# Low-half products of the first MLP half woven between the high-half products

## The chip, the cores and the metric

The kernel runs on one core of a Trainium2 chip. The metric is the device time of one execution in microseconds. Names used below: TensorE multiplies matrices (PE in the profile, with its weight loads on a row of their own, PEld), VectorE is DVE, ScalarE is ACT, GpSimd is POOL, and SyncE (SP) issues the loads from memory.

## The reference

One layer of a diffusion backbone: two token mixers (differential attention and multi-scale pooling) merged by gates, and then a squared-ReLU MLP. There are 256 latent tokens and 256 context tokens of 2048 channels; the MLP has 8192 hidden channels. Everything is in float32. What matters here is the last line:

```python
def sq_relu_mlp(h, w1, w2):
    return jnp.square(jax.nn.relu(h @ w1)) @ w2

x = x + ga * mix
x = x + gm * sq_relu_mlp(modulate(x, norm_mlp_w[l], sm, cm), w_ff1[l], w_ff2[l])
```

## The kernel before

**High and low halves.** TensorE multiplies in the type float32r, which keeps fewer bits than float32. So every operand is split in two: `hi` is the value rounded to float32r, `lo` the rounded rest, `value - hi`. A product of two float32 matrices is then three products: high by high, high by low, and low by high. Weights arrive in chunks of 128 x 1024 values in one of five `raw` tiles, by a DMA on SyncE's queue. ScalarE casts a chunk to `whi` (line 243, `act.copy(hi, raw)`), VectorE subtracts to get `wlo` (line 244); there are three `whi` and three `wlo` tiles. `wchunk` hands out the next chunk of a long list, `stream`, whose order is written out beforehand, and sees to it that two chunks beyond it have been asked for (`AHEAD = 2`). At a certain rate it also advances a side job, `late_gen`, which works out a modulation vector from weights of its own: it borrows a `raw` tile for each of them, and VectorE multiplies and adds it into `macc` (line 651).

**The MLP.** The hidden channels are worked through in eight blocks of 1024, numbered 0 to 7. `ff1_first` makes block 0. `ff1(b)` makes block b for 1 to 7 and `ff2(b)` multiplies the finished block with its part of the second weight matrix and adds to `acc`. They are called in the order `ff1(1)`, `ff2(0)`, `ff1(2)`, `ff2(1)`, and so on to `ff1(7)`, `ff2(6)`, `ff2(7)`. So a block that `ff1` finishes is read only one `ff2` later.

**`ff1`.** The weights are the stationary operand, 128 x 128 at a time, and the hidden state `h2` moves. For each of the block's eight columns of 128 channels (four pairs `i`, two halves `j`) there is one PSUM bank `ps` of 512 columns and there are two chunks of weights (`kc`), each with eight slices `kk`. Per chunk there are first eight high products: `both(h2, k)` is the high and the low half of `h2` side by side, 2 x 256 = 512 columns, so that one product gives high by high in the bank's first 256 columns and high by low in its last 256. Behind them come eight low products: the slice of `wlo` with the high half of `h2` alone, 256 columns, added to the bank's last 256. These are lines 1061 and 1064 (below called highs and lows). After both chunks ScalarE copies the last 256 columns out (`f1c`, line 1067) and VectorE adds the first 256 (`f1s`, line 1068). After two columns ScalarE takes the ReLU, GpSimd squares, and `split` (lines 270, 271) makes the high and low half of the block, `act`.

**`ff2` and the other stages.** `xstat` makes the products of `ff2` and of most other projections: the tokens are stationary, the weights move, 512 columns a product. Per chunk it gives, for `part == 0`, the high weights with the high and the low half of the tokens (lines 453 and 454, alternating), and for `part == 1` the low weights with the high half (line 459). In `ff2` that is eight and four products a chunk. The pooling stage uses `mm3` (lines 274 to 276) with products of 256 columns.

**Order.** The instructions are scheduled from the order of the text; on TensorE the profile shows the products of the MLP in the order of the text. Functions handed to `later` are called some chunks on, from `wchunk`.

Of the kernel before, what the change touches and what calls it, by code (L numbers as in the profile page):

```python
# [13 lines left out]
AF = mybir.ActivationFunctionType  # L14
# [3 lines left out]
P = 128  # L18
D = 2048
KT = D // P  # L20
T = 256
# [27 lines left out]
def layer(ctx: ExitStack, tc, a, out):  # L49
# [3 lines left out]
    pe, gp = nc.tensor, nc.gpsimd  # L53
# [15 lines left out]
    act, vec, pe, sp = Engine(nc.scalar, ordered), Engine(nc.vector, ordered), Engine(nc.tensor, ordered_pe), nc.sync  # L69

    def bank(name):
        return psum.tile([P, 512], F32, tag="ps", name=name)

    def work(name, shape=None, dt=F32):
        return pool.tile(shape or [P, 512], dt, tag="w2", name=name, bufs=9)

    def s16(name, shape, dt=F32):
        return pool.tile(shape, dt, tag="s16", name=name, bufs=7)
# [7 lines left out]
    def pairtile(name):  # L86
        return s16(name, [P, 2, 8, T], F32R)
# [8 lines left out]
    def later(n, fn):  # L96

        waiting.append([n, fn])
# [154 lines left out]
    def wchunk(*key, ahead=AHEAD):  # L253
        while len(loaded) < min(done[0] + 1 + ahead, len(stream)) or loaded[done[0]][1] is None:
            if loaded and done[0] < len(loaded) and loaded[done[0]][1] is None:
                done[0] += 1
                continue
            load_next()
        got, hi, lo = loaded[done[0]]
        assert got == key, (got, key)  # L260
        loaded[done[0]] = None
        done[0] += 1
        tick()
        return hi, lo
# [4 lines left out]
    def split(hi, lo, src):  # L269
        act.copy(hi, src)  # L270
        vec.tensor_sub(lo, src, hi.bitcast(F32))  # L271

    def mm3(o, l_hi, l_lo, r_hi, r_lo, start, stop):
        pe.matmul(o, l_hi, r_hi, start=start, stop=False)
        pe.matmul(o, l_hi, r_lo, start=False, stop=False)
        pe.matmul(o, l_lo, r_hi, start=False, stop=stop)
# [89 lines left out]
    def act_slice(tiles, k, part):  # L366
        return tiles[k // 8][:, part, k % 8, :]

    def both(tiles, k):
        return tiles[k // 8][:, :, k % 8, :]  # L370

    def tok(tiles, k, part, t):
        return tiles[k // 8][:, part, k % 8, t * P:t * P + P]
# [56 lines left out]
    def xmm(banks, toks, k, hi, lo, sl, first, last):  # L430
        for ps, (h, t) in zip(banks, toks):
            mm3(ps, tok(h, k, 0, t), tok(h, k, 1, t), hi[:, sl], lo[:, sl], first, last)

    def xstat(w, banks, toks, nk=8, last=1, more=0, held_back=None):

        for ch in range(nk - last + 1):
            n = last if ch == nk - last else 1  # L440
            chunks = [wchunk(*w, ch + i, ahead=max(AHEAD - i, more if i == last - 1 else 0)) for i in range(n)]
            order = [(i, kk, t) for i in range(n) for kk in range(2) for t in range(len(banks))]
            if ch == nk - last:
                order.sort(key=lambda o: o[2])
            groups = [order] if n == 1 else [[o for o in order if o[2] == t] for t in range(len(banks))]
            for group in groups:
                for part in range(2):
                    for i, kk, t in group:
                        k = 2 * (ch + i) + kk
                        h, tt = toks[t]  # L450
                        wt = chunks[i][part][:, kk * 512:kk * 512 + 512]
                        if part == 0:
                            pe.matmul(banks[t], tok(h, k, 0, tt), wt, start=k == 0, stop=False)  # L453
                            pe.matmul(banks[t], tok(h, k, 1, tt), wt, start=False, stop=False)  # L454
                        elif held_back is not None and group is groups[-1] and k >= 2 * nk - 3:
                            held_back.append(partial(pe.matmul, banks[t], tok(h, k, 0, tt), wt, start=False,
                                                     stop=k == 2 * nk - 1))
                        else:
                            pe.matmul(banks[t], tok(h, k, 0, tt), wt, start=False, stop=k == 2 * nk - 1)  # L459
            yield len(banks)  # L460
# [110 lines left out]
    for f in range(KT):  # L571
        if f % 2 == 0:
            ps = bank("mod")
# [109 lines left out]
    def v_group(g):  # L683
        bs = [bank(f"v{g}_{t}") for t in range(4)]
        for ch, w in enumerate(xstat(("w_v", g), bs, tokens(4))):

            yield w if g == 0 or ch > 1 else 2 * ch
        for t in range(4):
            act.copy(v[:, t, g * 512:g * 512 + 512], bs[t])
        values[0] += 4  # L690

    def k_group(g):
        bs = [bank(f"k{g}_{t}") for t in range(4)]
        for ch, w in enumerate(xstat(("w_k", g), bs, tokens(4))):
            if ch < 7:
                yield w
        for t in range(4):
            qk_evac(bs[t], t, g, kT, 2, 3 + t)
        yield w

    def q_group(g):
        bs = [bank(f"q{g}_{t}") for t in range(2)]
        for _ in xstat(("w_q", g), bs, tokens(2)):
            yield 0
        for t in range(2):
            qk_evac(bs[t], t, g, qT, 0, 4 + t)
# [243 lines left out]
    h2 = [pairtile("h2_0")]  # L950
# [25 lines left out]

    acc = s16("acc", [P, 2, D])
    acts = {}

    def ff1_first(wo):  # L980

# [54 lines left out]
        for h in range(2):  # L1036
# [5 lines left out]
                part.append(r)  # L1042
            later(3 + h, partial(turn4, at, 4 * h, part))

    def ff1(b):

        at = pairtile("act")  # L1050
        acts[b] = at
        for i in range(4):
            s = work("f1s")
            for j in range(2):
                f = 8 * b - 8 + 2 * i + j
                ps = bank("f1")
                for kc in range(2):
                    hi, lo = wchunk("w_ff1", f, kc)
                    for kk in range(8):
                        k = 8 * kc + kk  # L1060
                        pe.matmul(ps, hi[:, kk * P:kk * P + P], both(h2, k), start=k == 0, stop=False)  # L1061
                    for kk in range(8):
                        k = 8 * kc + kk
                        pe.matmul(ps[:, T:2 * T], lo[:, kk * P:kk * P + P], act_slice(h2, k, 0), start=False,  # L1064
                                  stop=k == KT - 1)
                c = work("f1c", [P, T])
                act.copy(c, ps[:, T:2 * T])
                vec.tensor_add(s[:, j * T:j * T + T], ps[:, 0:T], c)
            sq = work("rsq2")
            r = work("relu")  # L1070
            act.activation(r, s, AF.Relu)  # L1071
            gp.tensor_mul(sq, r, r)  # L1072
            split(at[:, 0, 2 * i:2 * i + 2, :], at[:, 1, 2 * i:2 * i + 2, :], sq.rearrange("p (a t) -> p a t", t=T))

    def ff2(b):
        at = [acts[b]]
# [20 lines left out]
    for b in range(8):  # L1097
        if b < 7:
            ff1(b + 1)
        else:  # L1100
            for g in range(4):
                gs = slice(g * 512, g * 512 + 512)
                for t in range(2):
                    gp.tensor_mul(acc[:, t, gs], acc[:, t, gs], mods["gm"][:, gs])
                    gp.tensor_add(acc[:, t, gs], acc[:, t, gs], x1[:, t, gs])
        ff2(b)
# [105 lines left out]
```

## Time and profile before

| what | value |
| --- | --- |
| median of 3 runs | 1470.62 us (1469.34 to 1471.14) |
| the profiled execution's own time | 1469.82 us |
| its span, first to last instruction | 1467.8 us |
| mean granted TensorE clock | 0.994 |
| TensorE busy (page, part 1) | 1437.1 us, 98% of the span |
| weight loads busy | 1183.6 us, 81% |
| VectorE, ScalarE, GpSimd busy | 1000.2, 683.5, 121.3 us |
| first line-1061 product to last (timeline) | 798.5 to 1374.9 us |

The page gives, in part 1, the time in which an engine was busy; in part 4 the chain of work that ended last, followed back from the end; in part 5 the costliest groups of instructions with their count, their busy time, the mean duration of one, and the engine's idle time before them. Durations of products overlap, because TensorE starts one before the last has drained: what a product costs is the distance from its start to that of the next. In the page a line such as `f<-h,whi` names the tile written and the tiles read; `ps` and `bs` of the MLP carry the name `f` there.

### The profile page before, as it was taken

What the parts mean: (1) busy time and instruction counts of PE and PEld (TensorE: products, weight loads), DVE (VectorE), ACT (ScalarE), POOL (GpSimd) and SP (SyncE); (2) the same over time, 40 slices, a digit from 0 to 9 for tenths busy, and PEclk for the clock granted to TensorE, in tenths of its full rate; (3) what the DMA queues carried; (4) which work ended last, traced back from release to release, by engine and by line L of the source; (5) the groups of instructions that cost most, each with busy time, mean ns of one, the idle gap of its engine ahead of it and who ended that gap; (6) DMA issues with size and microseconds to landing.
All of it is one profiled execution on the core that took longest, in us unless ns stands there. A gap on an engine that the chain in (4) does not pass through costs nothing.

```text
span 1467.8 us, 19774 instructions
## 1 busy us (share of the span) xinstructions
PE 1437.1 (98%) x7466; PEld 1183.6 (81%) x7466; DVE 1000.2 (68%) x1243; ACT 683.5 (47%) x929; POOL 121.3 (8%) x120
## 2 busy tenths in 40 slices
PE   4999999999999999999999999999999999999998
PEld 3667887778878888888888888888888888888887
DVE  4667787868887786768676656666666655555675
ACT  4334336466554344435444554445344453544442
POOL 0001110101400000000001000001000000000260
PEclk8999999999999999999999999999999999999999
DMA  9996585435788888899646777767777655555554
GB/s 364 409 408 237 198 284 178 144 115 167 226 289 293 297 274 305 279 310 323 206 168 204 231 245 233 238 224 235 238 239 241 201 189 193 191 190 194 185 195 141
DMA packets 97439, 347.85 MB, mean 237 GB/s; under 512 B 11072, under 2 KB 11712, under 8 KB 97344
## 3 DMA queue, kind: packets, MB, share of 16 engines
q1 hardware_dynamic: 96768, 345.51, 69.6%
q8 instruction: 58, 0.95, 0.3%
q0 software_dynamic: 576, 1.08, 0.2%
q14 instruction: 37, 0.30, 0.1%
HBM read 344.45 MB, written 2.10 MB: 236 GB/s over the span
## 4 chain that ended last, share of the span: by engine, by line
PE 91%; DVE 4%; ACT 2%; DMA 1%; issue 1%; POOL 0%; DVEq 0%; SPq 0%; ACTq 0%; POOLq 0%
PE f L1061 14%; PE f L454 8%; PE f L453 8%; PE f L459 8%; PE f L1064 7%; PE pg L454 4%; PE pg L453 4%; PE pg L459 4%; PE w_k L67 3%; PE wo L453 2%; PE wo L454 2%; PE pyy L453 2%; PE pyy L459 2%; PE pyy L454 2%; PE wo L459 2%; PE v L459 2%
## 5 line engine op out<-in xcount | busy, mean ns | idle before, releaser
L244 DVE TENSOR_TENSOR wlo<-raw,whi 128x1024 fp32r<-128x1024 f32 (+1 forms) x430 | 534.7, 1245 | 341.6 <-ACT whi L243 319.6
L243 ACT CAST whi<-raw 128x1024 fp32r<-128x1024 f32 (+1 forms) x430 | 449.6, 1047 | 551.7 <-PE f L454 179.6
L1061 PE MATMUL f<-h,whi 128*128 128x512 f32 x896 | 224.3, 392 | 0.0
L454 PE MATMUL f<-whi,act 128*128 128x512 f32 x512 | 199.3, 389 | 0.0
L453 PE MATMUL f<-whi,act 128*128 128x512 f32 x512 | 199.3, 389 | 0.0
L1061 PEld LDWEIGHTS f<-h,whi 128*128 128x128 f32 x896 | 161.6, 189 | 29.2
L651 DVE SCALAR_TENSOR_TENSOR macc<-raw,sil,macc 128x1024 f32<-128x1024 f32 x128 | 165.0, 1289 | 4.0 <-issue 2.5
L459 PE MATMUL f<-wlo,act 128*128 128x512 f32 x512 | 136.8, 389 | 0.0
L1064 PEld LDWEIGHTS f<-h,wlo 128*128 128x128 f32 x896 | 122.2, 190 | 8.7
L1064 PE MATMUL f<-h,wlo 128*128 128x256 f32 x896 | 124.9, 282 | 0.0
L459 PEld LDWEIGHTS f<-wlo,act 128*128 128x128 f32 x512 | 96.1, 188 | 20.0
L454 PEld LDWEIGHTS f<-whi,act 128*128 128x128 f32 x512 | 96.1, 188 | 19.8
L453 PEld LDWEIGHTS f<-whi,act 128*128 128x128 f32 x512 | 96.1, 188 | 19.8
L453 PE MATMUL pg<-whi,hL 128*128 128x512 f32 x256 | 101.4, 396 | 0.0
L454 PE MATMUL pg<-whi,hL 128*128 128x512 f32 x256 | 100.6, 393 | 0.0
L1072 POOL TENSOR_TENSOR rsq<-relu 128x512 f32<-128x512 f32 x28 | 29.2, 1043 | 527.5 <-ACT relu L1071 497.0
L459 PE MATMUL pg<-wlo,hL 128*128 128x512 f32 x256 | 68.6, 390 | 0.0
L454 PEld LDWEIGHTS pg<-whi,hL 128*128 128x128 f32 x256 | 48.5, 189 | 10.3 <-issue 0.2
L453 PEld LDWEIGHTS pg<-whi,hL 128*128 128x128 f32 x256 | 48.5, 189 | 10.3 <-issue 0.2
L459 PEld LDWEIGHTS pg<-wlo,hL 128*128 128x128 f32 x256 | 48.4, 189 | 10.1
L632 POOL MEMSET macc<- 128x1024 f32 x8 | 7.6, 955 | 479.2 <-DVE al L271 374.9
L1086 DVE TENSOR_TENSOR acc<-f,acc 128x512 f32<-128x512 f32 x48 | 30.9, 686 | 19.6 <-PE f L459 19.6
(275 smaller groups left out, 2098.1 us busy)
## 6 DMA issues: line engine op xcount, KB each, us to landing
raw<-in_w_ff_dram SPq DMA_DIRECT2D x240, 512.0 KB, 4.2
raw<-in_w_m_dram SPq DMA_DIRECT2D x64, 512.0 KB, 9.8
raw<-in_w_ga_dram SPq DMA_DIRECT2D x32, 512.0 KB, 4.6
raw<-in_w_cm_dram SPq DMA_DIRECT2D x32, 512.0 KB, 4.6
raw<-in_w_gb_in_dram SPq DMA_DIRECT2D x32, 512.0 KB, 4.7
raw<-in_w_ga_in_dram SPq DMA_DIRECT2D x32, 512.0 KB, 5.0
raw<-in_w_sm_dram SPq DMA_DIRECT2D x32, 512.0 KB, 4.9
raw<-in_w_o_dram SPq DMA_DIRECT2D x32, 512.0 KB, 4.6
```

What stands on the lines that cost most here:

```text
L67: return (lambda *a, **k: pin(emit(*a, **k))) if self.flag[0] else emit
L243: act.copy(hi, raw)
L244: vec.tensor_sub(lo, raw, hi.bitcast(F32))
L453: pe.matmul(banks[t], tok(h, k, 0, tt), wt, start=k == 0, stop=False)
L454: pe.matmul(banks[t], tok(h, k, 1, tt), wt, start=False, stop=False)
L459: pe.matmul(banks[t], tok(h, k, 0, tt), wt, start=False, stop=k == 2 * nk - 1)
L632: gp.memset(acc, 0.0)
L651: pin(vec.scalar_tensor_tensor(acc, raw, sil[:, 0, k:k + 1], acc, ALU.mult, ALU.add))
L1061: pe.matmul(ps, hi[:, kk * P:kk * P + P], both(h2, k), start=k == 0, stop=False)
L1064: pe.matmul(ps[:, T:2 * T], lo[:, kk * P:kk * P + P], act_slice(h2, k, 0), start=False, stop=k == KT - 1)
L1072: gp.tensor_mul(sq, r, r)
L1086: vec.tensor_add(acc[:, t, gs], bs[t], acc[:, t, gs])
```

## The change

The lows of `ff1` are no longer given out in runs of eight. Each is put into a list, `behind`, as its high is given out, and `weave(4)` gives out the oldest entry when the list holds more than four. So behind the first four highs of a block, high and low alternate, and each low comes four highs after the high of its own slice. This goes on across chunks and columns. The last four lows of a block are still in the list when `ff1` ends; `xstat`, in the `ff2` that follows, calls `weave(0)` behind each of its products with `part == 0`, and so they stand behind the first four of those. Elsewhere the list is empty and `weave` does nothing. What followed a column's last low (copy, addition, and after two columns ReLU, square and split) has moved into `ff1_out` and is given out behind that low, wherever it now stands. The number of instructions, their shapes and the list of loads are the same.

```diff
+    behind = []
+
+    def weave(lag):
+
+        if len(behind) > lag:
+            behind.pop(0)()
+
     def xstat(w, banks, toks, nk=8, last=1, more=0, held_back=None):
...
                             pe.matmul(banks[t], tok(h, k, 0, tt), wt, start=k == 0, stop=False)
+                            weave(0)
                             pe.matmul(banks[t], tok(h, k, 1, tt), wt, start=False, stop=False)
+                            weave(0)
...
+    halves = [None]
+    LAG = 4
...
+    def low_product(ps, lo, kk, k, done_with):
+
+        pe.matmul(ps[:, T:2 * T], lo[:, kk * P:kk * P + P], act_slice(h2, k, 0), start=False, stop=k == KT - 1)
+        if k == KT - 1:
+            done_with()
+
+    def ff1_out(b, i, j, ps):
+
+        if j == 0:
+            halves[0] = work("f1s")
+        s = halves[0]
+        c = work("f1c", [P, T])
+        act.copy(c, ps[:, T:2 * T])
+        vec.tensor_add(s[:, j * T:j * T + T], ps[:, 0:T], c)
+        if j == 1:
+            at = acts[b]
+            sq = work("rsq2")
+            r = work("relu")
+            act.activation(r, s, AF.Relu)
+            gp.tensor_mul(sq, r, r)
+            split(at[:, 0, 2 * i:2 * i + 2, :], at[:, 1, 2 * i:2 * i + 2, :], sq.rearrange("p (a t) -> p a t", t=T))
+
     def ff1(b):
-        at = pairtile("act")
-        acts[b] = at
+        acts[b] = pairtile("act")
         for i in range(4):
-            s = work("f1s")
             for j in range(2):
...
                         pe.matmul(ps, hi[:, kk * P:kk * P + P], both(h2, k), start=k == 0, stop=False)
-                    for kk in range(8):
-                        k = 8 * kc + kk
-                        pe.matmul(ps[:, T:2 * T], lo[:, kk * P:kk * P + P], act_slice(h2, k, 0), start=False,
-                                  stop=k == KT - 1)
-                c = work("f1c", [P, T])
-                act.copy(c, ps[:, T:2 * T])
-                vec.tensor_add(s[:, j * T:j * T + T], ps[:, 0:T], c)
-            sq = work("rsq2")
...
+                        behind.append(partial(low_product, ps, lo, kk, k, partial(ff1_out, b, i, j, ps)))
+                        weave(LAG)
```

More of the change, by code (lines that the diff above doesn't have):

```diff
@@ L1061, in ff1 @@
                         pe.matmul(ps, hi[:, kk * P:kk * P + P], both(h2, k), start=k == 0, stop=False)
-                    for kk in range(8):
-                        k = 8 * kc + kk
-                        pe.matmul(ps[:, T:2 * T], lo[:, kk * P:kk * P + P], act_slice(h2, k, 0), start=False,
-                                  stop=k == KT - 1)
-                c = work("f1c", [P, T])
-                act.copy(c, ps[:, T:2 * T])
-                vec.tensor_add(s[:, j * T:j * T + T], ps[:, 0:T], c)
-            sq = work("rsq2")
[L1070 to L1073, printed above, removed]
+                        behind.append(partial(low_product, ps, lo, kk, k, partial(ff1_out, b, i, j, ps)))
+                        weave(LAG)
     def ff2(b):
```

## The prediction

> **What bounds the kernel now.** I read the page first, for the share of each engine and the costliest groups; then the chain of waits around one block of the first MLP half; then the timeline, product by product, where a run of short products begins and ends.
>
> ```profile
> span 1467.8 us, 19774 instructions
> PE 1437.1 (98%) x7466; PEld 1183.6 (81%) x7466; DVE 1000.2 (68%) x1243; ACT 683.5 (47%) x929; POOL 121.3 (8%) x120
> ...
> PE 91%; DVE 4%; ACT 2%; DMA 1%; issue 1%; POOL 0%; DVEq 0%; SPq 0%; ACTq 0%; POOLq 0%
> ...
> L1061 PE MATMUL f<-h,whi 128*128 128x512 f32 x896 | 224.3, 392 | 0.0
> ...
> L1064 PE MATMUL f<-h,wlo 128*128 128x256 f32 x896 | 124.9, 282 | 0.0
> ```
>
> TensorE is busy 98% of the span and carries 91% of the chain that ended last. The two lines that the change moves, 896 high products of 512 columns and 896 low ones of 256, have no idle time before them. So the time of this stage is the sum of the distances from one product's start to the next. The mean durations (392 and 282 ns) overlap and say nothing of that; the chain of waits does. It is merged here for the stretch 885 to 940 us (start, length, line, count; its times lie 0.16 us behind the starts of the timeline, so only differences are used):
>
> ```profile
> 885.85 0.23 PE f L453
> ...
> 888.57 1.81 PE f L1061 x8
> 890.38 0.95 PE f L1064 x8
> 891.34 1.84 PE f L1061 x8
> 893.17 0.95 PE f L1064 x8
> ...
> 930.44 1.84 PE f L1061 x8
> 932.28 0.95 PE f L1064 x8
> 933.24 0.23 PE f L453
> ```
>
> Between 885.85 and 888.57 lie the twelve 512-column products of one chunk of the second MLP half: 2.72 us, or 226.7 ns each. Eight of that rate make 1.81 us, which is what the block's first eight highs take. Every later run of eight highs takes 1.84 us, and each run of eight lows 0.95 us, 119 ns each. One chunk (eight and eight) takes (930.44 - 891.34) / 14 = 2.793 us, or 349.1 ns for a pair of one high and one low.
>
> If a low took half of a high by its columns, it would take 113.3 ns, a pair 340.0 ns, a chunk 2.720 us. So 0.073 us of each chunk is lost. Where, the timeline of single products shows (start, length, engine, line; each of these rows is the answer to a narrow window, and a row of two starts at its first):
>
> ```profile
> 889.99 0.39 PE L1061 MATMUL f<-h,whi 128*128 128x512 f32 x1
> 890.22 0.28 PE L1064 MATMUL f<-h,wlo 128*128 128x256 f32 x1
> 890.33 0.40 PE L1064 MATMUL f<-h,wlo 128*128 128x256 f32 x2
> 890.45 0.40 PE L1064 MATMUL f<-h,wlo 128*128 128x256 f32 x2
> 890.57 0.40 PE L1064 MATMUL f<-h,wlo 128*128 128x256 f32 x2
> ...
> 890.22 0.19 PEld L1064 LDWEIGHTS f<-h,wlo 128*128 128x128 f32 x1
> 890.34 0.19 PEld L1064 LDWEIGHTS f<-h,wlo 128*128 128x128 f32 x1
> 890.45 0.19 PEld L1064 LDWEIGHTS f<-h,wlo 128*128 128x128 f32 x1
> ...
> 933.07 0.40 PE L453 MATMUL f<-whi,act 128*128 128x512 f32 x1
> ...
> 934.23 0.39 PE L454 MATMUL f<-whi,act 128*128 128x512 f32 x1
> ```
>
> The low that follows a high lasts 0.11 us (890.22 to 890.33); from the second on they last 0.12. Each weight load starts as the product before its own starts (load 890.22 beside product 890.22, load 890.34 beside product 890.33). So a load has exactly one product's length to hide in: behind a high it has 227 ns, behind a low 113. Back to back behind lows it takes 120, about 7 ns too much, seven times in a run: 0.047 us. The rest, 0.026 us, is the run of highs that follows (1.84 against 1.81): a high after a run of lows is slow for a while. The same is seen in the second half behind the block: five products from 933.07 to 934.23 take 1.16 us instead of 5 x 0.2267 = 1.133.
>
> **The change part by part.** Instructions, shapes and counts are the same; only the order of TensorE's products changes, and with it the moment at which buffers come free.
>
> Order: behind the first four highs of a block, high and low alternate; the last four lows of a block stand behind the first four products of the second half that follows. No low follows a low any more. The price of a pair is not in the trace as an alternating stream, so I bound it. From below: a high at its best rate (226.7) and a low at its best (113.3), 340.0 ns; no row above is faster. From above, the only place where highs stand between short products: two lone 512-column products inside the pooling's runs of 256 columns.
>
> ```profile
> 331.53 0.28 PE L276 MATMUL pin<-hL,wlo 128*128 128x256 f32 x1
> 331.65 0.40 PE L670 MATMUL late<-ah,ones 128*128 128x512 f32 x1
> 331.88 0.40 PE L671 MATMUL late<-al,ones 128*128 128x512 f32 x1
> 332.12 0.28 PE L274 MATMUL pin<-hL,whi 128*128 128x256 f32 x1
> 332.24 0.28 PE L275 MATMUL pin<-hL,whi 128*128 128x256 f32 x1
> 332.36 0.28 PE L276 MATMUL pin<-hL,wlo 128*128 128x256 f32 x1
> ```
>
> Those two take (332.12 - 331.65) / 2 = 235 ns, the 256s behind them 120: a pair of 355 ns, worse than the 349.1 of today. I take the lower end, 340. The reason is the row at 890.22: there a low stands behind a high that is at its best rate, as it does in the new order, and it takes 113. Behind the low comes a high whose load began as the low began, just as the load at 890.22 began, and that one was in time. The pooling's highs stand behind a run of 256s that had been waiting for their loads, a state which the new order never enters.
>
> The sum at that rate: fifteen chunks of a block give 0.073 each and the first, which has no slow highs, 2.77 - 2.72 = 0.05 (891.34 - 888.57), together 1.14 us; seven blocks 8.0 us. The slow products behind the seven blocks give 7 x 0.027 = 0.2. Gain 8.2 us. The profiled execution took 1469.82 us (its span and 2.0 us around it), so 1461.6 by its own measure; the median of the runs is 0.8 us above it, so 1462.4.
>
> Buffers: the last high of a chunk now begins 2.4 us into it instead of 1.6, so the cast that waits for the freed high tile (890.42 below, as the eighth high of its chunk ends) comes 0.8 us later. The last low ends 1.4 us into the next chunk (after three pairs, a high and itself), so the subtraction that fills the freed low tile starts at 1.4 us into that chunk, not 0.3. These hide behind work that is in the rows:
>
> ```profile
> 890.42 1.05 ACT L243 CAST whi<-raw 128x1024 fp32r<-128x1024 f32 x1 [0.70 <-PE f L1061]
> ...
> 888.78 1.23 DVE L244 TENSOR_TENSOR wlo<-raw,whi 128x1024 fp32r<-128x1024 f32 x1 [1.50 <-ACT whi L243]
> ...
> 890.04 0.33 SPq L116 DMA_DIRECT2D raw<-in_w_ff_dram  x1
> ...
> raw<-in_w_ff_dram SPq DMA_DIRECT2D x240, 512.0 KB, 4.2
> ...
> 898.80 1.05 ACT L243 CAST whi<-raw 128x1024 fp32r<-128x1024 f32 x1 [1.74 <-PE f L1061]
> ...
> 888.40:933.00 44.60, 44.60 (x257) 39.26 (x256) 28.66 (x30) 23.09 (x32) 3.13 (x3) 1.00 0.73 236
> ```
>
> With three buffers, a tile filled in the chunk after its release is read two chunks later. The subtraction would end at 1.4 + 1.2 = 2.6 us, the first low that reads it is at 2 x 2.72 + 1.6 = 7.0 us: 4.4 us to spare. What queues behind that subtraction on VectorE (the f1s additions, the accumulations of the late modulation) is read by nobody on TensorE for as long; VectorE is busy 28.66 of the block's 44.60 us and ScalarE 23.09. The raw buffer is released at the subtraction's end, and SyncE issues its next load at once (888.78 + 1.23 = 890.01, issue 890.04). It lands about 4.2 us later, at 894.2, and with five raw buffers, one of them lent to the late weights, its cast is the fourth from there, at 898.80: 4.6 us to spare, of which the later release takes 1.1. So SyncE's queue is moved by a microsecond and no cast waits for it. The copy, addition, ReLU and square of each column block come 1.4 us later; their PSUM bank is held that much longer, with eight banks and three or four in use. At a block's end they fall into the second half, and their result is read a whole stage (over 40 us) later. I cost all of this at nothing; if the cover were gone, each microsecond per chunk would cost 112 us.
>
> **A page weighed against a row.** In a run of lows the trace shows one load per 120 ns. The Trainium skill, "TensorE: Matmul & The Clock Gate", section "LDWEIGHTS (loading the stationary operand)", gives a load as its columns divided by 1.2, which is 107 ns for 128 columns. By that estimate a load fits into a low's 113 ns and the sum is the 8.2 us above; by the 120 of the row, if it holds behind a single low too, it is the second rival below. The same page, section "Step-by-step: what each phase is for", says that loads are pulled ahead into a background weight buffer; the loads of this trace, each starting with the product before its own, agree, and this speaks against the change: a low is too short to hide more than one load, wherever it stands.
>
> **The rivals.** First, on the other side: the highs never get back to their best rate. Each high stands behind a low, and every row of a high behind a run of lows is slow, as at 331.65. With 355 ns a pair the stage takes 896 x (355 - 349.1) = 5.3 us more: 1475.9. It decides as soon as a pair costs over 349.1. For it speaks that recovery took five highs at 933.07, and the new order never has two highs in a row; against it, that all such rows stand behind lows that had waited for loads.
>
> Second: the load of a high's weights needs 120 ns behind its low, as the loads at 890.34 and 890.45 do, while the highs keep 226.7. Pair 346.7, gain 896 x (349.1 - 346.7) = 2.2 us: 1468.4, no measurable change. Against it: the first low's 0.11.
>
> Third: the order on the chip isn't that of the text, because the lows find another place when the instructions are scheduled, or the two effects cancel: 1470.6. The order of before agrees with its text row by row (x8, x8), which speaks against.
>
> Fourth: a new wait. If the subtraction, now behind the last low, came 4.4 us too late, TensorE would stand; 0.1 us a chunk is 11.2 us, 1473.6 with the gain kept. The sums above speak against it.
>
> **How the numbers follow.** What a measurement here can tell from no change is about 0.2%, 2.9 us. The forecast has 0.46 (its own range 1461.0 to 1465), the slow highs 0.22, the bound load 0.20, no other order or a cancellation 0.08, a wait 0.04. Faster is the forecast alone, 0.46; same is the bound load and the third rival, 0.28; slower is the first and the fourth, 0.26. The range goes from the forecast by its best case, 1461.0, to the slow highs at 1476.0; beyond lies little but the wait.
>
> **What would show it.** In the chain of waits the runs x8 of both lines are gone, and a high and a low take 0.34 us together, 5.44 us for sixteen pairs; 0.347 is the bound load, 0.35 and above the slow highs. A block (now 933.24 - 888.57 = 44.67 us) takes 43.5. The high after a low is 0.227 apart from its successor if I am right, 0.233 to 0.236 if the first rival is. The first five products of the second half lose their 0.027. The idle time before both product lines stays 0.0; if not, a wait has come. The prediction is wrong if the slow state belongs to any change of length rather than to waiting loads.

## The result, and the profile after

The changed kernel takes 1473.48 us (median of 11 runs, 1471.13 to 1476.17); the kernel before took 1468.92 us in 11 runs beside them. The ratio is 1.0026, 95% interval 1.0015 to 1.0036: slower by a quarter of a per cent, some 3.8 us (the medians differ by 4.6), where 1462.4 was forecast. The profiled execution took 1473.48 us, with a span of 1471.5.

The page after, for the same groups as before, by engine, line, tile and shape, with count, busy time, mean ns of one, and idle time before it:

```profile
span 1471.5 us, 19748 instructions
PE 1441.5 (98%) x7466; PEld 1182.3 (80%) x7466; DVE 1000.3 (68%) x1243; ACT 685.1 (47%) x929; POOL 145.0 (10%) x120
...
L1089 PE MATMUL f<-h,whi 128*128 128x512 f32 x896 | 313.5, 398 | 0.0
L1058 PE MATMUL f<-h,wlo 128*128 128x256 f32 x896 | 251.6, 281 | 0.0
```

Lines 1089 and 1058 are the highs and lows that were lines 1061 and 1064. Their idle time is still 0.0: no wait has come. The whole loss is in the distances between products. The timeline of the same block shows them (start, length, engine, line):

```profile
889.83 0.28 PE L1058 MATMUL f<-h,wlo 128*128 128x256 f32 x1
889.94 0.40 PE L1089 MATMUL f<-h,whi 128*128 128x512 f32 x1
890.17 0.28 PE L1058 MATMUL f<-h,wlo 128*128 128x256 f32 x1
890.29 0.40 PE L1089 MATMUL f<-h,whi 128*128 128x512 f32 x1
890.53 0.28 PE L1058 MATMUL f<-h,wlo 128*128 128x256 f32 x1
890.65 0.40 PE L1089 MATMUL f<-h,whi 128*128 128x512 f32 x1
890.88 0.28 PE L1058 MATMUL f<-h,wlo 128*128 128x256 f32 x1
891.00 0.40 PE L1089 MATMUL f<-h,whi 128*128 128x512 f32 x1
...
892.06 0.40 PE L1089 MATMUL f<-h,whi 128*128 128x512 f32 x1
```

The order is the one in the text. But it repeats itself every three pairs: from 889.94 to 891.00, and again to 892.06, three highs and three lows take 1.06 us, 353.3 ns a pair. Before it was 349.1, and 340 was forecast. 896 x (353.3 - 349.1) = 3.8 us, which is the loss: the two profiled spans differ by 3.7. In the trace's nanoseconds the three highs take 232, 241 and 235, the lows behind them 118, 120 and 114; none of these highs takes 227. Behind the last low of the block the second half is slow as well (chain of waits; start, length, line):

```profile
934.97 0.24 PE f L460
935.21 0.24 PE f L462
...
935.68 0.23 PE f L462
```

So the 0.2 us that the forecast counted there did not come either. The slow stretch even grew: by the starts in the traces it costs 63 ns over ten products behind six of the seven blocks, where it cost 27 ns over five before.

The buffers moved about as worked out. In the chunk that starts with the high at 891.00, the cast and the subtraction are:

```profile
893.91 1.05 ACT L243 CAST whi<-raw 128x1024 fp32r<-128x1024 f32 x1 [1.77 <-DVE wlo L244]
...
892.66 1.23 DVE L244 TENSOR_TENSOR wlo<-raw,whi 128x1024 fp32r<-128x1024 f32 x1 [2.37 <-PE f L1058]
```

The cast comes 2.9 us into its chunk, as its last high ends (893.87 in the trace); before it came 2.0 us in (a chunk from 888.41, the cast at 890.42). The row puts the wait down to the subtraction, which ends at nearly the same moment, 893.89. With the lag of one, below, the subtraction ends at 894.05 and the cast, at 894.58, is put down to the high; so it is the high that it waits for. The subtraction waits for TensorE's last low of the chunk ahead, 1.66 us into this one.

One delay was not foreseen. GpSimd's square takes 1894 ns on the page after, 1043 on the page before; ScalarE's cast of its result waits for it, up to 2.2 us at a time, and a cast of weights queued behind that one comes late (at 906.66, though the high in its way ended at 905.17). TensorE doesn't feel it: its idle time is 0.0, and the run with short loads for the highs, below, has the square at 1850 ns and is fast all the same.

### The profile page after: what moved, and what is told of

It reads as the page before. It is cut to its first block, busy times and chain, and to the rows that moved or that the text cites. A ratio compares the mean times of both kernels' runs of the same rounds, so it can differ in the third digit from the quotient of the medians.

```text
span 1471.5 us, 19748 instructions
## 1 busy us (share of the span) xinstructions
PE 1441.5 (98%) x7466; PEld 1182.3 (80%) x7466; DVE 1000.3 (68%) x1243; ACT 685.1 (47%) x929; POOL 145.0 (10%) x120
## 4 chain that ended last, share of the span: by engine, by line
PE 87%; DVE 6%; DMA 3%; ACT 2%; issue 1%; POOL 0%; SPq 0%; DVEq 0%; ACTq 0%; POOLq 0%
PE f L1089 14%; PE f L460 8%; PE f L462 8%; PE f L468 8%; PE f L1058 7%; PE pg L460 3%; PE pg L462 3%; PE pg L468 3%; PE w_k L67 2%; PE wo L460 2%; PE wo L462 2%; PE wo L468 2%; PE pyy L462 2%; PE pyy L468 2%; PE pyy L460 2%; PE v L462 2%
## 5 line engine op out<-in xcount | busy, mean ns | idle before, releaser
L1089 PE MATMUL f<-h,whi 128*128 128x512 f32 x896 | 313.5, 398 | 0.0
L1058 PE MATMUL f<-h,wlo 128*128 128x256 f32 x896 | 251.6, 281 | 0.0
L1089 PEld LDWEIGHTS f<-h,whi 128*128 128x128 f32 x896 | 168.4, 188 | 41.7
L1058 PEld LDWEIGHTS f<-h,wlo 128*128 128x128 f32 x896 | 169.2, 189 | 0.3
L1075 POOL TENSOR_TENSOR rsq<-relu 128x512 f32<-128x512 f32 x28 | 53.0, 1894 | 510.6 <-ACT relu L1074 410.7
L271 DVE TENSOR_TENSOR act<-rsq,act 128x512 fp32r<-128x512 f32 x28 | 19.4, 693 | 44.4 <-ACT act L270 44.4
```

## The experiments

Times of single runs stand beside one run of the kernel before on the same chip, or beside the median of nine, and differ by a few microseconds from run to run. So the verdicts rest on the distances in the traces, which repeat. "Short" is a load of 64 stationary columns instead of 128.

**Is it the alternation of tiles and banks?** Lows of 512 columns:

```diff
-        pe.matmul(ps[:, T:2 * T], lo[...], act_slice(h2, k, 0), start=False, stop=k == KT - 1)
+        pe.matmul(ps, lo[...], both(h2, k), start=False, stop=k == KT - 1)
```

> The order of the changed kernel, with lows of 512 columns (the low weights times both halves of the hidden state), so that every product of the stage has the same length and only the tile of the weights alternates. Theory R (rhythm: a product is slow behind one of another length, whatever the loads do): all products settle at 226.7 ns, a pair at 453.3, time 1468.9 + 896 x (453.3 - 349.1) ns = about 1562 us. Theory L (load: a high is slow because its weights had to be loaded beside a short low): the same 453.3, since every load has 227 ns. Theory T (tiles or bank: taking turns between high and low weight tiles, or adding to a part and to the whole of a bank, costs by itself): at least the 13 ns a pair lost in the changed kernel stay, 467 ns, about 1574 us.

1563.59 us against 1472.54. The chain of waits:

```profile
904.78 0.23 PE f L1058
905.00 0.23 PE f L1089
...
906.82 0.23 PE f L1089
```

Nine products from 904.78 to 906.82 take 2.04 us, 226.7 ns each, highs and lows alike. Taking turns between two weight tiles costs nothing. Here the lows write the whole bank too, so this run says nothing of turns between the whole and a part of a bank; the next one does, where highs write the whole and lows a half, and lose nothing. The two together put theory T out. Theories R and L expected the same and are not told apart.

**Is it the high's load?** Woven order, 64 stationary columns in 15 of 16 highs:

```diff
+                        m = P if k == 0 else 64
-                        pe.matmul(ps, hi[:, kk * P:kk * P + P], both(h2, k), ...)
+                        pe.matmul(ps[0:m, :], hi[:, kk * P:kk * P + m], both(h2, k), ...)
```

> The order of the changed kernel, but 15 of 16 highs use 64 of their 128 stationary columns (half of the output channels are left out), so that the load that must fit beside a low is halved. Theory L: the load is in time and the pair falls from 353.3 to 340 ns, time about 1461 us. Theory R: lengths alternate as before, the pair stays near 353 ns, about 1473 us.

1463.65 us against 1472.54. Its timeline, with the one full load among sixteen at 909.34 (128*128); the last row is that load:

```profile
909.00 0.39 PE L1090 MATMUL f<-h,whi 128*64 128x512 f32 x1
909.23 0.28 PE L1058 MATMUL f<-h,wlo 128*128 128x256 f32 x1
909.34 0.40 PE L1090 MATMUL f<-h,whi 128*128 128x512 f32 x1
909.57 0.28 PE L1058 MATMUL f<-h,wlo 128*128 128x256 f32 x1
909.69 0.39 PE L1090 MATMUL f<-h,whi 128*64 128x512 f32 x1
909.92 0.28 PE L1058 MATMUL f<-h,wlo 128*128 128x256 f32 x1
910.03 0.39 PE L1090 MATMUL f<-h,whi 128*64 128x512 f32 x1
...
910.71 0.39 PE L1090 MATMUL f<-h,whi 128*64 128x512 f32 x1
...
909.23 0.19 PEld L1090 LDWEIGHTS f<-h,whi 128*128 128x128 f32 x1
```

With the short load a pair takes the 340 ns of the forecast (909.00 to 909.34; two pairs from 910.03 to 910.71 in 0.68), although lengths alternate: theory L expected this, theory R 353. And the fully loaded high shows how the loss is paid. The low in front of it, beside which its load ran, is as short as ever, 0.11 (909.23 to 909.34). What comes after is slow: the high and the low behind it take 0.35 (909.34 to 909.69), and the two pairs to 910.03 take 0.69; in the trace's nanoseconds 693 instead of 680, spread over the high (232), the low (118) and the next high (230). So here the late load does not hold back the start of its product; it makes the product itself, and the two behind it, longer. (A product with 64 stationary columns also uses half of the array. No run halves the load alone in float32r, but such products are no faster by themselves: with both at 64, in the next runs, a pair still takes 340 ns, which is the 226.7 of a full product of 512 columns and half of that.)

The other way round, 64 columns in the lows and 128 in the highs (`m = P if k == KT - 1 else 64` at the lows), and both at 64:

> The order of the changed kernel; now 15 of 16 lows use 64 of their 128 stationary columns (half of their channels left out) and the highs keep 128, so that the shorter load is the one beside a high. Theory S (share: every load takes time from the stream of the product beside it, in proportion to its columns, 13.3 ns for 128 and 6.7 for 64, wherever it stands): high 220, low 120, pair 340 ns, 8 us below the kernel before. Theory L (only the high's load beside the short low does harm): nothing changes for it, the pair stays at 353 ns, 4 us above. Theory R (unlike lengths alone): 353 as well, but the run with highs of 64 columns, at 340, already speaks against it.

> As the run with lows of 64 stationary columns, with 15 of 16 highs at 64 too. Theory S: high 220, low 113.3, pair 333.3 ns, 14 us below the kernel before. Theory L: all loads are in time, high 226.7 and low 113.3, pair 340, 8 us below.

1466.09 and 1461.85 us against 1469.09. From the chain of waits of the two, first the short lows alone, then both:

```profile
904.92 0.12 PE f L1059
905.04 0.23 PE f L1090
...
907.35 0.12 PE f L1059
```

```profile
905.01 0.11 PE f L1059
905.12 0.23 PE f L1091
...
906.71 0.11 PE f L1059
```

Seven pairs in 2.43 us are 347 ns, five pairs in 1.70 are 340. Short loads for both are no faster than short loads for the highs alone. So the load beside a high is free where nothing is late, and no load takes a fixed share of the stream: theory S is out, which expected 340 and 333. Theory L was right on the second, and wrong on the first, where it expected 353: with the high's load still late, a short load for the low behind it halves the loss.

**Is time enough for the load a cure?** Lows of 384 columns (two stretches of 192), beside which a load has 170 ns; then the same with 64 stationary columns for both; then with the 384 columns in one stretch:

```diff
+        pe.matmul(ps.rearrange("p (a t) -> p a t", t=T)[:, :, 0:192], lo[...], both(h2, k)[:, :, 0:192], ...)
```

> The order of the changed kernel, with lows of 384 columns (two stretches of 192: the lows reach 192 tokens in each half of the bank instead of all 256 in the second), so that a load beside a low has 170 ns instead of 113. Theory L: nothing is late, the pair is 226.7 + 170.0 = 397 ns, 1468.9 + 896 x (396.7 - 349.1) ns = about 1511.5 us. Theory R: the lengths still alternate and the highs stay at 232 to 241 ns, the pair is about 407 to 410 ns, 1520 to 1524 us.

> The alternating run with lows of 384 columns (two stretches of 192 tokens), now with 64 of 128 stationary columns in 15 of 16 highs and lows. So far: the run with short loads for both settled at 340 ns (no faster than short loads for the highs alone, so a load takes no fixed share of the stream, theory S is out); lows of 384 with full loads cost 407 instead of 397, though a load had 170 ns. Theory L (loads): short loads free this stream too, pair 397 ns, 43 us above the kernel before. Theory G (length: a product of 384 columns puts the stream off its beat, whatever is loaded): 405 ns or more, 50 us above or more.

> As the alternating run with lows of 384 columns and 64 stationary columns for both, but the 384 columns are one stretch (they run on into the next slice of the hidden state, so the lows add other values), not two of 192. If the two stretches cost the 8 ns a pair lost there (404.5 instead of 396.7), the pair falls to 397 ns, 43 us above before. Theory G (a length of 384 puts the stream off its beat): it stays at 404 or 405, 49 us above.

1520.82 against 1472.54, 1521.51 against a median of 1470.74, and 1520.17 against 1468.01 us. The chain of waits of the first run, then of the third:

```profile
904.90 0.23 PE f L1090
...
907.35 0.23 PE f L1090
```

```profile
904.96 0.17 PE f L1059
...
907.38 0.17 PE f L1059
```

Six pairs take 2.45 and 2.42 us: 408 ns a pair with full loads (407 in the trace's nanoseconds), 403 with short ones (405 over the whole stage, where one load in sixteen is full), not 397. One stretch or two makes no difference: by the starts in the traces, over the whole stage, the second run takes 404.7 ns a pair and so does the third. So lows of 384 columns cost 7 to 11 ns a pair, most of it for a reason that isn't a late load. Theory R had the first run right and theory G the other two; theory L was wrong in the first two, and the two stretches are not the cause either.

Runs of eight with 384 columns never settled either:

> The order of before (runs of eight) with lows of 384 columns (two stretches of 192 tokens, as in the alternating run with 384), full loads. Theory S: lows settle at 160 + 13.3 = 173.3 ns. If instead the stream has a fixed pace by column (226.7 / 512), they settle at 170.0, and no load is late, so the highs behind lose nothing. By S the highs behind a run are slow here as well if that belongs to the change of length, 5 us more or less of the stage: 8 highs and 8 lows at 3.200 us plus up to 0.03.

1524.24 against 1469.09 us. Eight lows take 1.42 us (chain of waits), 178 ns each, not 173 or 170, and the eight highs behind them 1.85:

```profile
905.85 1.42 PE f L1064 x8
907.26 1.85 PE f L1061 x8
```

**Whose are the slow highs behind a run of lows?** Runs of eight, first with short lows (`m` as above, at the lows of the kernel before), then with a short load for the one high that stands behind every second run (`m = 64 if k == 8 else P`):

> The order of before (runs of eight), but 15 of 16 lows use 64 of their 128 stationary columns (half of their output channels left out). Theory L: the loads no longer bound the run, lows take 113 ns, the slow highs behind the run go, a chunk falls from 2.793 to 2.720 us, time about 1461 us. Theory R: 120 ns is the pace at which a run of 256-column products settles; lows stay at 120, the highs behind stay slow, a chunk stays at 2.79 us, about 1469 us.

> The order of before (runs of eight), but the first high behind every second run of lows (the first of a column's second chunk) uses 64 of its 128 stationary columns. Theory L (the cost of a late load is paid by the product it belongs to and the ones behind it, not by the product beside which it runs): the load of that high is in time, its five slow highs (234, 235, 228, 232, 231 ns) go back to about 227, while those of the column's first chunk stay slow; 56 x 0.027 us = 1.5 us below the kernel before. Rival (the stream is slow for a while behind any run of lows, whatever the load): both chunks alike, as before.

1465.26 against 1472.54, and 1469.34 against 1468.01 us. The chain of waits of the first, then of the second:

```profile
904.17 1.84 PE f L1061 x8
906.01 0.92 PE f L1065 x8
```

```profile
905.88 1.84 PE f L1062 x8
907.72 0.95 PE f L1065 x8
908.66 1.82 PE f L1062 x8
```

Short lows run at 0.92 us instead of 0.95, so the 120 ns of a run of lows are its loads; but the highs behind, whose first is loaded in full beside the last low, stay at 1.84. With that one load short, as in the second run, the eight highs take 1.82 where the column's other eight take 1.84; undisturbed eight take 1.81. So most of the tail belongs to the one late load, as theory L had it, and about a third does not: in the trace's nanoseconds the high with the short load still takes 233 and the one behind it 231, and only the three behind those, which were slow too, are back at 227. So theory L had the lows of the first run right but not its chunk: 2.76 us, where it expected 2.720 and theory R 2.79. The 1.5 us that theory L expected of the second run's time are too little to be seen between two single runs.

**Lag and run length.** A lag of one instead of four, runs of two, and runs of sixteen (`LAG = 1`; the loop over `kk` cut into steps of two; the lows of both chunks behind the highs of both):

> The changed kernel with a lag of one instead of four: each low stands behind the high of the next slice. Theory L and G alike: the order of lengths and loads on TensorE is the same, the pair stays at 353 ns, 4 us above before. Rival (buffers freed later, by the lag): between before and the changed kernel.

> Nothing left out: highs and lows in runs of two instead of eight. Theory S with a loss at each return to the highs: the changed kernel loses 6.7 ns per return over 346.7 a pair, runs of eight 20 ns per return. If the loss per return is 6.7, a pair takes 350 ns, 1 us above before; if it is 20, 356.7 ns, 7 us above. Theory L: the low behind a high is free and the second of each two waits for its load, so (340 + 346.7) / 2 = 343.3 and 5 us below before.

> Nothing left out: both chunks' highs (sixteen), then both chunks' lows (sixteen), so that there is one return from lows to highs where there were two. Theory L with a loss at each return (27 ns in the highs behind a run of lows, in whatever length of run): a column block falls from 2 x 2.793 = 5.587 to 5.566 us, 1.2 us in all, too little to be seen in the time; seen in the trace, a block of 16 chunks is 0.17 us shorter. Rival: the loss grows with the run, and nothing is gained.

1473.72 against 1468.01, 1470.05 against 1469.09, and 1469.72 against a median of 1470.74 us. From the chain of waits of the three, in this order:

```profile
904.90 0.24 PE f L1089
...
905.96 0.24 PE f L1089
...
907.02 0.24 PE f L1089
```

```profile
905.41 0.47 PE f L1062 x2
...
907.50 0.46 PE f L1062 x2
```

```profile
895.04 3.65 PE f L1063 x16
898.70 1.91 PE f L1065 x16
900.61 3.65 PE f L1063 x16
```

The lag does nothing: again 1.06 us for three pairs. Runs of two take 2.09 us for six pairs, 348 ns a pair, a shade under the 349.1 of runs of eight; of the expected 343, 350 and 357 the middle one came nearest. Runs of sixteen take 5.57 us a column, as expected, against 5.587. So the loss per low does not rise step by step with the number of returns: it is 13 ns when lows stand alone, 8 in twos, 9 in eights, 8 in sixteens.

**Short loads with nothing left out.** Lows in bfloat16, in runs of sixteen and woven:

```diff
+            lo = pool.tile([P, n], BF16 if key[0] == "w_ff1" else F32R, tag="wlo", name="wlo", bufs=3)
+    h2b = s8("h2b", [P, KT, T], BF16)
+        gp.tensor_copy(h2b[:, 2 * kp:2 * kp + 2, sl], hi.bitcast(F32))
-        ... act_slice(h2, k, 0) ...
+        ... h2b[:, k, :] ...
```

> As the runs of sixteen, but the lows of this stage are computed in bfloat16: VectorE writes the low weights in it, and GpSimd makes one bfloat16 copy of the hidden state's high half, which takes the place of the moving operand. Theory L: a load of half the bytes is no longer than a low, lows take 113 ns or less in the whole run, and one return in sixteen is all that is lost: two chunks in 16 x 226.7 + 16 x 113.3 + about 40 ns = 5.48 us instead of 5.587, 6 us below the kernel before. Rival: a load costs by its columns, not its bytes, lows stay at 120, 1 us below; or the change of type costs at each return, and it is slower.

> The order of the changed kernel with the same bfloat16 lows. Theory L: the load beside a high becomes short, the one beside a low stays a full float32r load and comes 6.7 ns late each time, as in the run with lows of 64 stationary columns: pair 346.7 ns, 2 us below the kernel before (not to be told from no change). Rival: highs stay at 232 to 241 ns because they alternate with another length, pair about 350 ns or more, no gain or slower.

The runs of sixteen take 1461.38 us against 1470.74: ratio 0.9941, interval 0.9928 to 0.9953. The woven order takes 1478.74: ratio 1.0058, interval 1.0044 to 1.0071. Chain of waits, first in runs, then woven:

```profile
898.07 1.76 PE f L1068 x16
899.83 3.67 PE f L1066 x16
903.50 1.76 PE f L1068 x16
```

```profile
904.90 0.12 PE f L1061
...
906.69 0.13 PE f L1061
```

In runs a low takes 110 ns and a column 5.43 us (898.07 to 903.50; 5.48 was expected) against 5.587 before: 56 x 0.157 = 8.8 us, near the 9.4 between the medians. A bfloat16 load lasts 98 ns on the page, a float32r one 188; but the products are in another type as well, so the load is not the only thing that changed. What the narrower type does to the result is not weighed here. Woven, five pairs take 1.79 us, 358 ns a pair, where theory L expected 346.7: the rival's number came, about 350 or more, but not for its reason, since mere change of length costs nothing at 256 columns (340 with short loads). A low now takes 0.12 to 0.13 us, where in runs it takes 0.11. The high's full load still runs beside a short low here, so the run doesn't show how much of the loss is the change of type and how much the late load. The kernel with runs of sixteen beats both the kernel before and the changed one.

## Why the prediction was wrong

- **The bounds and the floor** held. 340 ns a pair exists (short high loads), 355 was the upper end, 353.3 came.
- **The step that failed** is the reason for taking the lower end: "Behind the low comes a high whose load began as the low began, just as the load at 890.22 began, and that one was in time." The load at 890.22 belongs to the product that starts at 890.33. That product starts on time, but it lasts 0.12 (890.33 to 890.45), not 0.11. So the load was late, and the row that shows it is the next one. I had read a product's distance to its successor as the verdict on the successor's load; the experiment with one full load in sixteen shows it as the verdict on its own: the low in front stays at 114 ns, the high with the full load takes 232. The low behind a high takes 113 ns because its own load ran beside that high. In the changed kernel no high that stands between lows takes the forecast's 227: they take 232, 241 and 235, and the pair 353.3 instead of 340.
- So the woven order keeps one late load per pair, the high's, and a late load that stands alone costs 13 ns over the next three products. A run of eight lows has eight late loads too (those of its last seven lows and of the high behind it), but together they cost 73 ns, about 9 each. The change took away the cheap form and put in the dear one.
- **The first rival**, slow highs at 1475.9, was nearest, at 355 ns instead of 353.3, and what it said of the highs came true: none gets back to its best rate. If the cause were the change of length alone, as the prediction's last sentence has it, the pair would not take 340 with short loads at the same lengths; so for 256 columns that cause is out. What the forecast held against it, a state that the new order never enters, was wrong as well.
- **The second rival**, a high's load of 120 ns behind its low at 346.7 a pair, named the right load but priced half of it: it counted the 6.7 ns by which the load is late and not what the next products lose. The same sum, 347, came where the low's own load was short, but that is luck: there the high's load was as late as ever, and the runs do not say why it cost half.
- **The page and the row.** The Trainium skill, "TensorE: Matmul & The Clock Gate", section "LDWEIGHTS (loading the stationary operand)", has a load take its columns divided by 1.2. The weight loads agree with that as a slope: 188 ns for 128 columns, 134 for 64, so 54 ns for 64 columns, where the page's rule gives 53.3. But the 107 ns that it gives for 128 columns would have fitted into a low's 113, and a load of 128 does not: the pair takes 353.3 ns with it and 340 with 64. The measurement decides.
- **The buffers** were right: the cast 0.9 us later (0.8 expected), the subtraction 1.66 us into a chunk (1.4 expected), and no idle time on TensorE, so the fourth rival, a wait, did not come. That ScalarE would wait for the square was not in the sum, but costing it at nothing was right. The lag of one, which frees buffers sooner, leaves the pair as it is.
- **The slow products behind the blocks** (0.2 us) stayed and grew, from 27 to 63 ns a block. That the product behind the last low is loaded in full beside it would explain that they stayed; why the stretch is longer now is not shown.

What stays open: why lows of 384 columns cost 7 or 8 ns a pair even with short loads and in one stretch; why a short load of the low halves the cost of the high's late one; the third of the tail that remains when the first high's load is short, the high itself at 233 ns; and what a change of type costs by itself.

## What to carry to other kernels

Where a product leaves too little time for the next weight load (113 ns for one that needs 120 here), look at the product whose load it was: in the run with one full load in sixteen, lateness showed in that product's own distance to the next, not in its start. Do not spread short products one by one between long ones to hide their loads without measuring a pair; here each then exposed the long one's load, and a low standing alone cost more (13 ns) than in a run (8 to 9). What helped is a shorter load: the lows in bfloat16, in long runs, took 8.8 us off the stage.

## What the runs showed of the hardware

- A stream of float32r products of 512 columns runs at 226.7 ns each, and one of 512 and 256 in turn at 340 ns a pair if the loads beside the short ones have 64 columns, whether those beside the long ones have 128 or 64; with 128 beside both it takes 353.3.
- bfloat16 lows of 256 columns take 110 ns in runs (1.76 us for sixteen) where float32r takes 120 (1.91). The Trainium skill, "TensorE: Matmul & The Clock Gate", section "Back-to-back issue gap", gives columns / 2.4 + 2.5 ns for what it calls the isolated gap at full clock, by that estimate 109 ns. The trace agrees for bfloat16, and not for float32r.
- Taking turns between bfloat16 and float32r costs 358 ns a pair, more than the same turns in float32r (353).
